# Fourteen column pairs per MLP in seven products, and their accumulated sums a product later

## The chip, the cores and the metric

The kernel runs on one core of one Trainium2 chip. A core has TensorE (PE; its weight loads are listed apart as PEld), VectorE (DVE), ScalarE (ACT), GpSimd (POOL) and SyncE (SP), which work side by side and wait for each other by semaphores. The metric is the device time of one execution in microseconds (us). The median of three runs of the kernel before is 2265.04 us (2263.68 to 2265.47).

## The reference

A decoder trunk of two layers on 256 tokens of width 2048, all in float32. Each layer adds a mixer (attention and a scan in layer 0, dilated attention in layer 1) and then an MLP:

```python
def squared_relu_mlp(h, w_up, w_down):
    u = jnp.einsum('bsd,df->bsf', h, w_up)
    return jnp.einsum('bsf,fd->bsd', jnp.square(jax.nn.relu(u)), w_down)

for layer in range(DEPTH):
    ...
    h = rms_norm(x, norm_ffn[layer])
    x = x + squared_relu_mlp(h, w_up[layer], w_down[layer])
```

`w_up` is 2048 x 8192 and `w_down` 8192 x 2048 in each layer. The change touches the MLPs alone.

## The kernel before

**Products in three parts.** Every large weight is split into a high part `whi` (a ScalarE copy) and the rest `wlo` (a VectorE subtraction), and so are the activations (`uh`, `ul` for u, the squared relu; `sh`, `sl` for sums of u). A product is three matmuls: high x high, high x rest, rest x high. Nearly all engine calls go through one helper, so the profile shows them under L71; tile names tell them apart.

**Pieces.** The work is one list, `plan`, of pieces of two k-tiles (256 rows of a weight, 512 columns, 512 KB). `run` walks it. In the iteration of piece i it first emits `low(i+2)` (VectorE's `wlo`), `fetch(i+6)` (SP's load), `high(i+3)` (ScalarE's `whi`), `add(i+4)` (a sum of weight blocks on VectorE), then what the piece before left pending (evictions), then the piece's matmuls. There are four `wlo` and five `whi` buffers. All engines work through their instructions in the order in which they were emitted.

**Up and down.** The hidden width of 8192 is 16 stripes of 512. An up unit makes one stripe of u in 8 pieces of 12 matmuls (`acc<-whi,hThi`). Behind it a side task `squared` takes relu (ScalarE), transposes (PE, `uT`), squares (ScalarE, `uf`). A second one, `operands`, splits a pair of stripes and makes the sums s1, s2. A plain down unit multiplies a pair c of stripes (c = 0 to 7) with 512 columns of `w_down` in 4 pieces of 12 matmuls (`acc<-whi,uh`).

**Seven products.** Instead of two plain down units (two column stripes of one pair c), a `Seven` takes the 2 x 2 blocks (two token tiles, two halves of the pair, two column stripes) with seven products in place of eight, in the Strassen-Winograd manner. Each product has two pieces of six matmuls (`sp<-`). Table `SEVEN` (L240) sets their order, each with its PSUM bank a, b or c and its weight block. `LOADS` says which blocks are loaded by SP with which product, `SUMS` which are summed on VectorE (`sraw<-sraw`). Two further sums (block 11 + block 12, and 12 + 22) are made by accumulating DMAs on POOL's queue, whose tile is also `sraw` (L276). A bank goes on accumulating over its products; after each product it is added to the residual (`res<-res,sp`) before the next product writes to it.

**Order.** `mixed` spreads the pieces of sevens among pieces of up units. Pair 6 and pair 7 stand last. Before, 12 sevens and 8 plain down units make up a layer: pairs 0, 1, 3, 4, 5 have two sevens each, pairs 2 and 6 one seven and two plain units, pair 7 four plain units.

**Side tasks.** A side task advances at a tick, twice per plain or up piece and once per product piece, as long as a running account of VectorE's and ScalarE's load is under `LIMIT`. A product's tick first books `HEAVY`, as much as `LIMIT`, so that no task runs there. What a piece needs and is not there yet is forced at that piece by `need`: the rest of the task's instructions are then emitted at once, ahead of the piece's matmuls.

Of the kernel before, what the change touches and what calls it, by code (L numbers as in the profile page):

```python
# [20 lines left out]
W = 512  # L21
# [19 lines left out]
def trunk(ctx: ExitStack, tc: tile.TileContext, x, norm_mix, norm_ffn, w_up, w_down, ab_w_in, ab_q_norm,  # L41
# [193 lines left out]
    def unit(*a, **k):  # L235
# [1 line left out]

    SEVEN = (("P1", "a", "11"), ("P2", "b", "21"), ("Q6", "a", "t2"), ("Q7", "c", "12"), ("Q5", "a", "11"),  # L240
             ("Q4", "c", "21"), ("Q3", "a", "22"))
    LOADS = {"P1": ("11",), "P2": ("21", "12", "22")}
    SUMS = {"Q6": ("t2", "11", "22"), "Q4": ("21", "21", "t2")}

    class Seven:


        def __init__(self, w, rows, c0, kts, operands, to, needs, mark):
            self.w, self.rows, self.c0, self.operands, self.to, self.needs, self.mark = \
                w, rows, c0, operands, to, needs, mark  # L250
# [8 lines left out]
        def fetch(self, p, h):  # L259
            for b in LOADS.get(SEVEN[p][0], ()):  # L260
                r, c = self.rows[int(b[0]) - 1] + h * KC, self.c0 + (int(b[1]) - 1) * W
                nc.sync.dma_start(self.tile(b, h),
                                  self.w[r * 128:(r + KC) * 128, c:c + W].rearrange("(k p) c -> p k c", p=128))

        def add(self, p, h):
            if SEVEN[p][0] in SUMS:
# [4 lines left out]
        def accumulate(self, p, h):  # L271

            o = {"P1": ("11", 0), "P2": ("12", 1)}.get(SEVEN[p][0])
            if o is not None:
                r, c = self.rows[o[1]] + h * KC, self.c0 + W
                nc.gpsimd.dma_start(self.raw[o[0], h],  # L276
                                    self.w[r * 128:(r + KC) * 128, c:c + W].rearrange("(k p) c -> p k c", p=128),
                                    accum_op=OP.add)

        def source(self, p, h):  # L280
            return self.raw[SEVEN[p][2], h]
# [1 line left out]
        def evict(self, p):  # L283

            name, b, _ = SEVEN[p]
            t, j, op = {"P1": (0, 0, OP.add), "P2": (0, 0, OP.add), "Q6": (1, 0, OP.add), "Q7": (1, 1, OP.subtract),
                        "Q5": (1, 1, OP.subtract), "Q4": (1, 0, OP.add), "Q3": (0, 1, OP.subtract)}[name]
            r = self.to[t][j]
            V.tensor_tensor(r, r, self.bank[b], op=op)

    def run():
        todo = plan
# [31 lines left out]
        def low(i):  # L324
            if i < len(todo):
                raw = raws.pop(i)
                lo = wpool.tile([128, KC, raw.shape[2]], F32R, name="wlo", bufs=AHEAD + 1)
                V.tensor_tensor(lo, raw, f32(parts[i][0]), op=OP.subtract)
                parts[i].append(lo)
                u, c = todo[i]  # L330
                if isinstance(u, Seven):
                    u.accumulate(*c)

        for i in range(RAW):
            if i % 2 == 0:
# [285 lines left out]
                last(t, j)  # L621
        free(ps)

    def residual_unit(w, ktiles, j, needs={}, nm=None, last=None, check=None, mark=None):
        def after(ps):
            if check is not None:
                check()
# [323 lines left out]
    def mlp(layer, nm, nxt, last=None):  # L951
# [60 lines left out]
        def down(c, j):  # L1012
            kts = [(4 * (2 * c + b) + k, (lambda b=b, k=k: u[2 * c + b] + (k,))) for b in range(2) for k in range(4)]
            marks[c].append(("down", layer, c, j))
            if c < NC - 1:
                return residual_unit(wd, kts, j, {4 * b: ("u", layer, 2 * c + b) for b in range(2)},
                                     mark=marks[c][-1]).pieces

            def whole():
                assert all(("down", layer, k, j) in done or ("down", layer, k, j - j % 2) in done for k in range(NC - 1))  # L1020

            return residual_unit(wd, kts, j, {4 * b: ("u", layer, 2 * c + b) for b in range(2)}, nxt, last, whole).pieces

        def seven(c, j):
            def parts(name):
# [5 lines left out]
            return Seven(wd, (8 * c, 8 * c + 4), j * W, 4, parts,  # L1031
                         [[res[:, t, (j + i) * W:(j + i + 1) * W] for i in range(2)] for t in range(2)],
                         {0: ("u", layer, 2 * c), 1: ("u", layer, 2 * c + 1), 2: ("sums", layer, c)},
                         marks[c][-1]).pieces

        def mixed(rest, s, start, end):

# [20 lines left out]

    n2 = Norm(R_MIX + 16, False)
    mlp(0, n1, n2)  # L1060
# [111 lines left out]
```

## Time and profile before

| | |
|---|---|
| median of 3 runs | 2265.04 us |
| profiled execution, its own time | 2264.74 us |
| its span, first to last instruction | 2262.9 us |
| PE, DVE, ACT busy in the span | 99%, 77%, 57% |
| chain of waits, share of PE | 97% |
| MLP of layer 0, about 515 to 1180 us | DVE 551.89 us busy, DMA share 0.81 |
| MLP of layer 1, about 1600 to 2263 us | DVE 540.62 us busy, DMA share 0.80 |
| granted TensorE clock | 1.00 |

A row of the timeline has its start, its duration, engine, line, operation, out<-in, the shape, a count, and in brackets the idle time of the engine before it with what ended that. Busy times of neighbouring matmuls overlap: the step from start to start tells what one costs. A row of the chain of waits has start, length and what ran.

### The profile page before, as it was taken

The page shows a single profiled execution, that of the slowest core. Times are in us where ns is not written, and L with a number is a line of the kernel's source. Part 1 is how long each engine was busy: PE and PEld are TensorE (multiplying, and loading weights), DVE is VectorE, ACT ScalarE, POOL GpSimd, SP SyncE. Part 2 cuts the span into 40 slices and gives each one's busy share as a digit, 9 for nine tenths or more (in the row PEclk, how much of TensorE's full clock was granted, in tenths as well). Part 3 has the DMA queues.
Part 4 walks back from the last instruction along what each step waited for, and adds up shares of the span by engine and source line. Part 5 has one row for each costly group of instructions (what it writes and reads, how often), then busy time and mean ns, then how long its engine had stood idle before and what let it go on. Part 6 is the DMA issues. An engine that isn't in the chain of part 4 may idle for free.

```text
span 2262.9 us, 30235 instructions
## 1 busy us (share of the span) xinstructions
PE 2247.2 (99%) x11029; PEld 1873.0 (83%) x11029; DVE 1749.7 (77%) x2482; ACT 1290.0 (57%) x1615; POOL 125.7 (6%) x116
## 2 busy tenths in 40 slices
PE   8999999999999999999999999999999999999999
PEld 7998988888888888888788778778888888888877
DVE  6779986556888888887976766665588888888786
ACT  6565545445666556565664555555566665656663
POOL 1000000000001010000000000000000000010000
PEclk9999999999999999999999999999999999999999
DMA  7546555568797797888756455546788789797874
GB/s 235 163 142 190 177 177 182 190 186 246 216 296 214 209 288 222 242 245 234 219 171 192 149 158 168 168 151 186 245 237 240 206 242 281 207 282 228 248 222 141
DMA packets 255318, 475.10 MB, mean 210 GB/s; under 512 B 17156, under 2 KB 27696, under 8 KB 255168
## 3 DMA queue, kind: packets, MB, share of 16 engines
q1 hardware_dynamic: 218976, 416.34, 56.7%
q0 software_dynamic: 26624, 50.48, 12.5%
q10 hardware_dynamic: 9568, 6.34, 0.9%
q8 instruction: 86, 1.41, 0.2%
q14 instruction: 64, 0.52, 0.1%
HBM read 470.97 MB, written 2.13 MB: 209 GB/s over the span
## 4 chain that ended last, share of the span: by engine, by line
PE 97%; DMA 1%; DVE 1%; issue 1%; ACT 0%; SPq 0%; DVEq 0%; POOLq 0%; ACTq 0%
PE acc L71 71%; PE sp L71 20%; PE uT L71 1%; PE sc L71 1%; PE o L71 1%; DMA sraw<-in_w_down_dram 1%; PE pT L71 1%; PE yp L71 1%; PE xT L71 1%; DVE wlo L71 1%; DMA wraw<-in_ab_w_in_dram 0%; PE qp L71 0%; DMA res<-in_x_dram 0%; PE yo L71 0%; PE kp L71 0%
## 5 line engine op out<-in xcount | busy, mean ns | idle before, releaser
L71 ACT ACTIVATE whi<-wraw 128x1024 fp32r<-128x1024 f32 (+1 forms) x600 | 631.9, 1054 | 493.6 <-PE acc L71 350.8
L71 DVE TENSOR_TENSOR wlo<-wraw,whi 128x1024 fp32r<-128x1024 f32 (+1 forms) x600 | 725.0, 1214 | 233.7 <-PE acc L71 159.7
L71 PE MATMUL acc<-whi,hThi 128*128 128x512 f32 (+1 forms) x1632 | 647.7, 397 | 1.8 <-ACT hThi L71 1.7
L71 PE MATMUL acc<-whi,hTlo 128*128 128x512 f32 (+1 forms) x1632 | 634.8, 389 | 1.0 <-DVE hTlo L71 1.0
L71 PE MATMUL acc<-wlo,hThi 128*128 128x512 f32 (+1 forms) x1632 | 634.1, 389 | 0.7 <-DVE wlo L71 0.7
L71 ACT ACTIVATE whi<-sraw 128x1024 fp32r<-128x1024 f32 x336 | 353.7, 1059 | 292.4 <-DVE sraw L71 137.0
L71 DVE TENSOR_TENSOR wlo<-sraw,whi 128x1024 fp32r<-128x1024 f32 x336 | 408.8, 1221 | 85.3 <-PE acc L71 35.3
L71 PEld LDWEIGHTS acc<-whi,hThi 128*128 128x128 f32 x1632 | 307.6, 188 | 66.8 <-issue 5.8
L71 PEld LDWEIGHTS acc<-whi,hTlo 128*128 128x128 f32 x1632 | 307.2, 188 | 65.7 <-DVE hTlo L71 1.8
L71 PEld LDWEIGHTS acc<-wlo,hThi 128*128 128x128 f32 x1632 | 307.9, 189 | 60.9 <-DVE wlo L71 1.1
L276 POOL DMA_DIRECT2D sraw<-in_w_down_dram x96 | 117.3, 1576 | 2058.7 <-DVE wlo L71 1815.6
L71 PE MATMUL sp<-wlo,sh 128*128 128x512 f32 x384 | 149.5, 389 | 0.0
L71 PE MATMUL sp<-whi,sl 128*128 128x512 f32 x384 | 149.5, 389 | 0.0
L71 PE MATMUL sp<-whi,sh 128*128 128x512 f32 x384 | 149.4, 389 | 0.0
L71 DVE TENSOR_TENSOR sraw<-sraw 128x1024 f32<-128x1024 f32 x96 | 117.1, 1219 | 26.4 <-DMA sraw<-in_w_down_dram 26.3
L71 DVE TENSOR_TENSOR res<-res,sp 128x512 f32<-128x512 f32 x168 | 114.7, 682 | 17.4 <-PE sp L71 17.1
L71 PE MATMUL acc<-hThi,whi 128*128 128x256 f32 x384 | 112.3, 293 | 0.0
L71 PE MATMUL sp<-whi,ul 128*128 128x512 f32 x288 | 112.1, 389 | 0.0
L71 PE MATMUL sp<-whi,uh 128*128 128x512 f32 x288 | 112.0, 389 | 0.0
L71 PE MATMUL sp<-wlo,uh 128*128 128x512 f32 x288 | 112.0, 389 | 0.0
L71 PE MATMUL acc<-hThi,wlo 128*128 128x256 f32 x384 | 108.5, 283 | 0.0
L71 PE MATMUL acc<-hTlo,whi 128*128 128x256 f32 x384 | 108.5, 283 | 0.0
(221 smaller groups left out, 2749.8 us busy)
## 6 DMA issues: line engine op xcount, KB each, us to landing
wraw<-in_w_up_dram SPq DMA_DIRECT2D x256, 512.0 KB, 5.2
sraw<-in_w_down_dram SPq DMA_DIRECT2D x192, 512.0 KB, 8.1
wraw<-in_ab_w_in_dram SPq DMA_DIRECT2D x96, 512.0 KB, 3.7
sraw<-in_w_down_dram POOLq DMA_DIRECT2D x96, 512.0 KB, 10.7
wraw<-in_c_w_qkv_dram SPq DMA_DIRECT2D x96, 512.0 KB, 4.2
wraw<-in_w_down_dram SPq DMA_DIRECT2D x64, 512.0 KB, 4.2
wraw<-in_ab_w_out_dram SPq DMA_DIRECT2D x48, 512.0 KB, 3.7
wraw<-in_c_w_o_dram SPq DMA_DIRECT2D x32, 512.0 KB, 3.6
```

The costliest lines, as they stand in the source:

```text
L71: return f(out, *a, **k)
L276: nc.gpsimd.dma_start(self.raw[o[0], h], self.w[r * 128:(r + KC) * 128, c:c + W].rearrange("(k p) c -> p k c", p=128), accum_op=OP.add)
```

## The change

Per layer 14 sevens (two for each of the pairs 0 to 6) and four plain down units (pair 7) take the place of 12 and 8. Further:

- The order of the products becomes P1, P2, Q7, Q6, Q5, Q4, Q3 (Q6 and Q7 change places).
- Block 12 is loaded together with block 11, with P1, and its accumulation with block 22 is issued on POOL's queue right behind its load. Block 11 is accumulated as before, after the subtraction of P1's piece.
- `operands` of pair 6 waits for pair 5's down work, and no longer for the end of all up units.
- The last two up units' pieces and the plain units of pair 7 are mixed anew with pair 6's sevens.
- A column's last step (norm of the next stage in layer 0, store in layer 1) starts when both its plain unit of pair 7 and its seven of pair 6 are through.

```diff
-    SEVEN = (("P1", "a", "11"), ("P2", "b", "21"), ("Q6", "a", "t2"), ("Q7", "c", "12"), ("Q5", "a", "11"),
+    SEVEN = (("P1", "a", "11"), ("P2", "b", "21"), ("Q7", "c", "12"), ("Q6", "a", "t2"), ("Q5", "a", "11"),
              ("Q4", "c", "21"), ("Q3", "a", "22"))
-    LOADS = {"P1": ("11",), "P2": ("21", "12", "22")}
+    LOADS = {"P1": ("12", "11"), "P2": ("21", "22")}
...
                 nc.sync.dma_start(self.tile(b, h),
                                   self.w[r * 128:(r + KC) * 128, c:c + W].rearrange("(k p) c -> p k c", p=128))
+                if b == "12":
+                    self.accumulate("12", 1, h)
...
-                if isinstance(u, Seven):
-                    u.accumulate(*c)
+                if isinstance(u, Seven) and c[0] == 0:
+                    u.accumulate("11", 0, c[1])
...
-            for k in marks[c - 1] if 0 < c < NC - 2 else [("up", layer)] if c else []:
+            for k in marks[c - 1] if 0 < c < NC - 1 else [("up", layer)] if c else []:
                 yield from until(k)
...
+        def ready(j, stored=True):
+
+            if early[j] == 2:
+                if last is not None and stored:
+                    for t in range(2):
+                        last(t, j)
+                if nxt is not None:
+                    nxt.begin(j)
...
-        for c, n in enumerate((20, 20, 8, 20, 20, 24, 0)):
+        for c, n in enumerate((18, 17, 17, 18, 17, 17, 8)):
             x, o = ups[o:o + n], o + n
+            s = seven(c, 0) + seven(c, 2)
             if c == NC - 2:
-                x = sum((down(c, j) for j in (0, 1)), []) + sum((down(c + 1, j) for j in range(NS)), [])
-                mixed(x, seven(c, 2), 2, 19)
-            elif n == 8:
-                mixed(x + down(c, 2) + down(c, 3), seven(c, 0), 4.5, 16)
+                mixed(x, s[:9], 4, n + 4)
+                mixed(sum((down(c + 1, j) for j in range(NS)), []), s[9:], 0, 15)
             else:
-                mixed(x, seven(c, 0) + seven(c, 2), 4.5, n + (3 if n == 24 else 0))
+                mixed(x, s, 4.5, n)
```

**Where instructions move: VectorE behind the last up piece.** In the changed kernel, layer 0, Q7 (bank sp_9828), Q6 and Q5 (both in bank sp_9705) and the first pieces of pair 7 (wlo_9869, wlo_9893) stand on VectorE like this; whi_9826 with wlo_9835 is Q6's second piece, wlo_9845 and wlo_9858 belong to Q5.

```order
L71 TENSOR_TENSOR res_82<-res_82,sp_9828 128x512
L71 TENSOR_TENSOR wlo_9858<-sraw_9589,whi_9849 128x1024
L71 TENSOR_TENSOR sraw_9646<-sraw_9646,sraw_9795 128x1024
L71 TENSOR_TENSOR wlo_9869<-wraw_9824,whi_9860 128x1024
L71 TENSOR_TENSOR res_82<-res_82,sp_9705 128x512
L71 TENSOR_TENSOR wlo_9882<-sraw_9646,whi_9873 128x1024
L71 TENSOR_TENSOR sraw_9699<-sraw_9699,sraw_9807 128x1024
L71 TENSOR_TENSOR wlo_9893<-wraw_9847,whi_9884 128x1024
L71 TENSOR_TENSOR res_82<-res_82,sp_9705 128x512
L71 TENSOR_TENSOR ul_9919<-uf_9631,uh_9918 128x1024
```

Q6's eviction, which Q5's first matmul waits for, stands behind two subtractions and a sum; before, Q7 stood between Q6 and Q5.

**ScalarE at the first plain unit of pair 7.** Its operand is uh_9918; relu_9902 and uf_9905 are of the last up unit, whose squares `operands` waits for. whi_9897 is the piece three ahead of the unit's first (whi_9860). The changed kernel:

```order
L71 ACTIVATE whi_9860<-wraw_9824 128x1024
L71 ACTIVATE whi_9873<-sraw_9646 128x1024
L71 ACTIVATE whi_9884<-wraw_9847 128x1024
L71 ACTIVATE whi_9897<-sraw_9699 128x1024
L71 ACTIVATE relu_9902<-acc_9594,rs32_4976 128x512
L71 ACTIVATE relu_9902<-acc_9595,rs32_4976 128x512
L71 ACTIVATE uf_9905<-uT_9906 128x512
L71 ACTIVATE uf_9905<-uT_9912 128x512
L71 ACTIVATE uh_9918<-uf_9631 128x1024
L71 ACTIVATE uh_9928<-uf_9905 128x1024
```

The kernel before, at the first plain unit of pair 6 (whi_9686, operand uh_9729, made from squares that are there):

```order
L71 ACTIVATE whi_9686<-wraw_9641 128x1024
L71 ACTIVATE whi_9698<-wraw_9653 128x1024
L71 ACTIVATE whi_9711<-sraw_9672 128x1024
L71 ACTIVATE whi_9724<-wraw_9684 128x1024
L71 ACTIVATE uh_9729<-uf_8903 128x1024
L71 ACTIVATE relu_9733<-acc_9409,rs32_4976 128x512
L71 ACTIVATE relu_9733<-acc_9410,rs32_4976 128x512
```

Before, uh stands ahead of the relu; now it stands behind relu, two transposes and two squares.

**PE at the same place of the changed kernel.** whi_9849 is the last product piece ahead of the unit (Q5).

```order
L71 MATMUL sp_9705<-whi_9849,sh_9676 128x512
L71 MATMUL sp_9705<-wlo_9858,sh_9676 128x512
L71 MATMUL sp_9705<-whi_9849,sl_9677 128x512
L71 MATMUL uT_9906<-cst_78,relu_9902 128x128 x4
L71 MATMUL uT_9912<-cst_78,relu_9902 128x128 x4
L71 MATMUL acc_9900<-whi_9860,uh_9918 128x512
L71 MATMUL acc_9900<-wlo_9869,uh_9918 128x512
L71 MATMUL acc_9900<-whi_9860,ul_9919 128x512
```

The last up unit's transposes stand directly between that product and the unit.

More of the change, by code (lines that the diff above doesn't have):

```diff
@@ L269, in add, with accumulate @@
                 V.tensor_tensor(self.raw[o, h] if o != "t2" else self.tile(o, h), x, y, op=OP.add)
[L271 to L278, printed above, removed]
+        def accumulate(self, b, half, h):
+            r, c = self.rows[half] + h * KC, self.c0 + W
+            nc.gpsimd.dma_start(self.raw[b, h],
+                                self.w[r * 128:(r + KC) * 128, c:c + W].rearrange("(k p) c -> p k c", p=128),
+                                accum_op=OP.add)
         def source(self, p, h):
@@ L289, in evict @@
             V.tensor_tensor(r, r, self.bank[b], op=op)
+            if p == 6 and self.after is not None:
+                self.after()
     def run():
@@ L622, in add_stripe, with residual_unit @@
         free(ps)
-    def residual_unit(w, ktiles, j, needs={}, nm=None, last=None, check=None, mark=None):
+    def residual_unit(w, ktiles, j, needs={}, nm=None, last=None, mark=None):
         def after(ps):
-            if check is not None:
-                check()
             add_stripe(ps, j, last)
@@ L1017, in down, with after, sevens_end @@
                                      mark=marks[c][-1]).pieces
-            def whole():
-                assert all(("down", layer, k, j) in done or ("down", layer, k, j - j % 2) in done for k in range(NC - 1))
-            return residual_unit(wd, kts, j, {4 * b: ("u", layer, 2 * c + b) for b in range(2)}, nxt, last, whole).pieces
+            def after(ps):
+                if early[j]:
+                    add_stripe(ps, j, last)
+                else:
+                    add_stripe(ps, j)
+                early[j] += 1
+                ready(j, False)
+            return Unit([(wd, j * W, W)], kts, after,
+                        needs={4 * b: ("u", layer, 2 * c + b) for b in range(2)}).pieces
+        early = [0] * NS
+        def ready(j, stored=True):
[5 more added lines that the diff above has]
+                    nxt.begin(j)
+        def sevens_end(j):
+            for k in (j, j + 1):
+                early[k] += 1
+                ready(k)
         def seven(c, j):
@@ L1033, in seven @@
                          {0: ("u", layer, 2 * c), 1: ("u", layer, 2 * c + 1), 2: ("sums", layer, c)},
-                         marks[c][-1]).pieces
+                         marks[c][-1], (lambda: sevens_end(j)) if c == NC - 2 else None).pieces
         def mixed(rest, s, start, end):
```

6 lines of the change are left out of this document (3 added, 3 removed).

## The prediction

> **What bounds the kernel now.** I read the page first: how busy each engine is, and which chain ends last.
>
> ```profile
> span 2262.9 us, 30235 instructions
> PE 2247.2 (99%) x11029; PEld 1873.0 (83%) x11029; DVE 1749.7 (77%) x2482; ACT 1290.0 (57%) x1615; POOL 125.7 (6%) x116
> PE 97%; DMA 1%; DVE 1%; issue 1%; ACT 0%; SPq 0%; DVEq 0%; POOLq 0%; ACTq 0%
> ```
>
> TensorE is the bound, with 97% of the chain. A matmul's busy time overlaps its successor's, so its true price is its step, from long runs in the chain of waits (start, length, count) and from the windows that hold the two MLPs (length, then PE, PEld, DVE, ACT, POOL busy, clock, DMA share, GB/s).
>
> ```profile
> 394.31 29.95 PE acc L71 x132
> 515.00:1180.00 665.00, 663.67 (x3002) 548.95 (x3001) 551.89 (x546) 404.72 (x442) 58.65 (x48) 1.00 0.81 235
> 1600.00:2263.00 663.00, 656.81 (x2953) 542.22 (x2951) 540.62 (x522) 390.16 (x408) 58.60 (x48) 1.00 0.80 233
> ```
>
> 29.95 / 132 = 0.227 us per 128x512 matmul. VectorE's 551.89 of 665 is 83%: second, with room. So the time moves by matmuls removed and by places where PE waits. Last I asked the timeline where PE waits inside the MLPs. In each layer the first plain down unit does so; PE rows of layer 0, then of layer 1:
>
> ```profile
> 1081.49 0.39 PE L71 MATMUL sp<-whi,sl 128*128 128x512 f32 x1
> 1082.62 0.50 PE L71 MATMUL acc<-whi,uh 128*128 128x512 f32 x1 [0.74 <-ACT uh L71]
> 1082.96 0.39 PE L71 MATMUL acc<-wlo,uh 128*128 128x512 f32 x1
> 1083.94 0.50 PE L71 MATMUL acc<-whi,ul 128*128 128x512 f32 x1 [0.59 <-DVE ul L71]
> 2170.97 0.39 PE L71 MATMUL sp<-whi,sl 128*128 128x512 f32 x1
> 2172.09 0.50 PE L71 MATMUL acc<-whi,uh 128*128 128x512 f32 x1 [0.74 <-ACT uh L71]
> ```
>
> Beyond the step PE loses 1082.62 - 1081.49 - 0.23 = 0.90 us for uh and 1083.94 - 1082.96 - 0.23 = 0.75 for ul: 1.65 per layer.
>
> **The change, part 1: fewer matmuls.** A pair of plain columns costs 2 units x 8 k-tiles x 2 token tiles x 3 = 96 matmuls, seven products 7 x 4 x 3 = 84. Two more such pairs per layer, two layers: 4 x 12 = 48 matmuls, 48 x 0.227 = **-10.9 us**, all on the bound engine.
>
> **Part 2: what they add elsewhere.** Each exchange adds 6 pieces to split (14 instead of 8), 4 weight sums, 3 evictions and 4 accumulating DMAs. The steps of VectorE and ScalarE come from starts that follow each other:
>
> ```profile
> 1067.93 1.22 DVE L71 TENSOR_TENSOR sraw<-sraw 128x1024 f32<-128x1024 f32 x1
> 1068.12 0.39 PE L71 MATMUL acc<-whi,hThi 128*128 128x512 f32 x1
> 1069.07 0.68 DVE L71 TENSOR_TENSOR res<-res,sp 128x512 f32<-128x512 f32 x1
> 1069.27 1.06 ACT L71 ACTIVATE whi<-sraw 128x1024 fp32r<-128x1024 f32 x1 [1.24 <-DVE sraw L71]
> 1069.66 1.22 DVE L71 TENSOR_TENSOR wlo<-wraw,whi 128x1024 fp32r<-128x1024 f32 x1
> ```
>
> A 128x1024 subtraction or sum keeps VectorE 1.14 us (67.93 to 69.07), an eviction 0.59; from a sum's start to the split that reads it pass 1.34. So 4 x (10 x 1.14 + 3 x 0.59) = 53 us more VectorE and 4 x 6 copies more ScalarE. They hide under PE: one up piece with two pieces of products is 24 x 0.227 = 5.45 us of PE against 3 x 1.14 + 0.65 (8 sums per 28 pieces) + 0.59 = 4.66 on VectorE, 86%. I count nothing; were that cover gone, VectorE would set each such group.
>
> **Part 3: the stall at the old place goes.** Its units become products, and the split of their u starts a stage earlier: 2 x 1.65 = **-3.3 us**.
>
> **Part 4: a longer stall at a new place.** The first plain unit now reads u of pair 14/15, and stands six pieces of products behind the last up piece. Ticks of products run no side task, so that whole chain (relu, transposes, squares, split) stands at the unit itself, behind the ScalarE split of piece whi_9897, which waits for a sum on VectorE. Also Q5 now follows Q6 directly there, both in bank sp_9705, so Q5 waits for Q6's eviction. Prices of the chain, from two stretches of the timeline:
>
> ```profile
> 1081.53 1.04 ACT L71 ACTIVATE uh<-uf 128x1024 fp32r<-128x1024 f32 x1
> 1082.47 1.25 ACT L71 ACTIVATE relu<-acc,rs 128x512 f32<-128x512 f32 x2
> 1082.67 1.22 DVE L71 TENSOR_TENSOR ul<-uf,uh 128x1024 fp32r<-128x1024 f32 x1
> 1843.98 0.39 PE L71 MATMUL sp<-whi,sl 128*128 128x512 f32 x1
> 1844.21 0.60 PE L71 MATMUL uT<-cst,relu 128*128 128x128 f32 x4
> 1844.40 0.69 DVE L71 TENSOR_TENSOR res<-res,sp 128x512 f32<-128x512 f32 x1 [0.29 <-PE sp L71]
> 1844.56 0.48 PE L71 MATMUL acc<-whi,uh 128*128 128x512 f32 x1
> 1844.84 0.60 ACT L71 ACTIVATE uf<-uT 128x512 f32<-128x512 f32 x1
> 1845.34 1.05 ACT L71 ACTIVATE whi<-wraw 128x1024 fp32r<-128x1024 f32 x1
> ```
>
> A copy of 128x1024 keeps ScalarE 0.94; the two relus end 1.25 after they start; four transposes keep PE 0.35, and the square follows 0.63 after their start, the next ScalarE step 0.50 later; uh's start to the unit's first matmul is 1.09 (1081.53 to 1082.62); an eviction starts 0.19 after the product's last step.
>
> Take the start of the last up piece as 0. An up piece is 2.72 us, a product piece 1.36, so Q7 ends at 5.44 and Q6 at 8.16. VectorE is at its best held by its four wlo buffers; it evicts Q7 at 5.63, and then in the order shown ahead: wlo_9858 at 6.22, sum sraw_9646 at 7.36, wlo_9869 at 8.50, Q6's eviction at 9.64. Q5 can start at 9.64 + 0.68 = 10.32 and ends at 13.04. VectorE goes on: wlo_9882 at 10.23, sum sraw_9699 at 11.37. ScalarE: whi_9897 at 11.37 + 1.34 = 12.71, relus 13.65 to 14.90, first square 0.52 later (three transposes are left then) at 15.42, second 15.92, uh 16.42, first matmul of the unit 17.51. Without waits it would start at 10.88 + 2 x 0.35 = 11.58. That is 5.9 us, and the wait for ul behind it stays 0.75: **6.7 us per layer, +13.4**.
>
> From below: if VectorE had nothing else, Q6's eviction ends at 9.03, Q5h0 at 10.39 frees whi_9897's buffer, and the same chain reaches the unit at 15.19: 3.6 + 0.75 = 4.4 per layer, 8.7. From above: VectorE has been late with an eviction today:
>
> ```profile
> 816.66 0.39 PE L71 MATMUL sp<-whi,sh 128*128 128x512 f32 x1
> 820.37 0.68 DVE L71 TENSOR_TENSOR res<-res,sp 128x512 f32<-128x512 f32 x1
> ```
>
> This one (Q6's) ended 4.39 us after the next piece had started. As late as 2.7 us beyond my chain makes 9.4 per layer, 18.8. I take 13.4, since buffers, not guesses, fix its start.
>
> **Part 5: more room for the accumulated sums.** Waits of VectorE for them, and the two late subtractions that PE felt:
>
> ```profile
> DVE sraw L71 <- DMA sraw<-in_w_down_dram: 26.3, 17, 4.3
> 1901.10 0.39 PE L71 MATMUL acc<-whi,hThi 128*128 128x512 f32 x1
> 1902.16 0.50 PE L71 MATMUL acc<-wlo,hThi 128*128 128x512 f32 x1 [0.67 <-DVE wlo L71]
> 2202.60 0.39 PE L71 MATMUL acc<-whi,uh 128*128 128x512 f32 x1
> 2203.40 0.50 PE L71 MATMUL acc<-wlo,uh 128*128 128x512 f32 x1 [0.42 <-DVE wlo L71]
> q0 software_dynamic: 26624, 50.48, 12.5%
> ```
>
> VectorE waited 26.3 us, but of it PE felt at most 0.83 + 0.57 = 1.4, the rest lies under its lead of three pieces. Between 0 and 1.4, I take **-0.7**. The 16 added accumulations (96 now) raise q0's share by about a sixth, 2% of the span; the windows above have 19% of the DMA engines' time free to hide it. P1's own block now queues behind another load; six pieces of lead (over 10 us) cover that.
>
> **Part 6: the end of the stage.** Norm and stores of a column now start when both its down unit and its seven are through. The third column's norm so begins one down piece before the end; its operand is needed at the fifth piece of the next unit, 4 x 2.72 = 10.9 us after that end, and it takes eight transposes, four copies and four subtractions of the size in this row of the groups (count, busy, mean ns, idle):
>
> ```profile
> L71 ACT ACTIVATE hThi<-xT,gains 128x256 fp32r<-128x256 f32 x64 | 26.0, 463 | 0.1
> ```
>
> Four times 0.46 us lie under PE's pieces: nothing. If they did not, PE would wait some 2 us once, since layer 1 has no norm behind it.
>
> **Sum.** -10.9 - 3.3 + 13.4 - 0.7 = -1.5. The profiled execution took 2264.74 (its span and 1.84 around it), 0.3 under the median of 2265.04; so 2263.2 like with like, **2263.5** against the median. A difference under 0.2%, 4.5 us, cannot be told from none here. From the bounds: -10.9 - 3.3 + 8.7 - 1.4 = -6.9 and -10.9 - 3.3 + 18.8 = +4.6, so 2258.5 to 2269.5 for this case alone.
>
> **The rivals.** *The new stall costs no more than the old one* (1.65 per layer): -10.9 - 0.7 = -11.6, 2253.5. For it: ScalarE is 57% busy and could be ahead. Against: the two waits stand in its queue and in PE's by program order, whatever the load. Chance 0.12.
>
> *The shared bank stalls the other sevens too.* Q5 follows Q6 through bank a in all 28; in 26 an up or down piece of 2.72 us stands between. It decides from an eviction that ends later than that. At 1069.07 above one stands directly behind a sum, as Q6's now will, and ends 1069.75 - 1068.12 = 1.63 after the next piece began: it fits. The one at 820.37 would not: 4.39 - 2.72 = 1.7 us. If a third of the 26 were late by that, 15 us: 2278. Against: that lateness came with the late accumulations that get more room. Chance 0.13.
>
> *The clock gate.* At the program's start matmuls of 128x288 step at 0.24 us, later at 0.13, until PE had worked for some 6 us (7.98 to 13.97):
>
> ```profile
> 13.25 0.44 PE L71 MATMUL acc<-wlo,hThi 128*128 128x288 f32 x1
> 13.49 0.44 PE L71 MATMUL acc<-whi,hTlo 128*128 128x288 f32 x1
> 18.32 0.29 PE L71 MATMUL acc<-whi,hTlo 128*128 128x288 f32 x1
> 18.45 0.30 PE L71 MATMUL acc<-whi,hThi 128*128 128x288 f32 x1
> ```
>
> If the new stall brought the slow step back for 6 us, each layer would lose 6 x (1 - 0.13 / 0.24) = 2.7, 5.4 in all: 2269. Against: no gap of my chain is over 2.2 us (8.16 to 10.32), and the windows' granted clock is 1.00. The Trainium skill, page "TensorE: Matmul & The Clock Gate", section "HAM oscillation — how this bites in real kernels", sets the limit at PE gaps over about 3.4 us; by that rule the forecast stands as long as no single gap passes it, and the slow start in the rows above agrees with its cold state. Chance 0.05.
>
> **Chances.** Forecast 0.70, the rivals 0.12, 0.13, 0.05. The forecast's own tails give 0.03 to faster and 0.02 to slower, the clock gate 0.01 to slower: faster 0.15, same 0.69, slower 0.16. With 0.25 on the outer rivals the range must reach into both: down to a new stall of 3.7 us per layer (2257.5), up to evictions late in four or five of the 26 places (4 x 1.7 = 7 us, 2270.5, and a little): **2257.5 to 2271.5**.
>
> **What would show it.** 48 matmuls fewer at the same step; no wait for uh at the first down unit's old place; in each layer one cluster of PE gaps of 6 to 7 us between the last up piece and the next plain unit, released by VectorE's eviction, ScalarE's relu and uh, and ul; VectorE's wait for accumulations well under 26.3; no new PE waits on res in the other sevens. I am wrong if that cluster is under 4 us or over 9.5 per layer, or if PE waits elsewhere by more than 3 us.

## The result, and the profile after

The changed kernel takes **2365.33 us** (median of 4 runs, 2362.71 to 2365.93) against 2264.81 (4 runs) for the kernel before: ratio 1.0444, 95% interval 1.0431 to 1.0456. It is 100 us slower, where the prediction said no difference.

The page of the changed kernel, the rows that answer those of before: the span, the busy times, and the shares of the chain that ended last. Then the windows of its two MLPs (length, PE, PEld, DVE, ACT, POOL busy, clock, DMA share, GB/s).

```profile
span 2363.7 us, 30362 instructions
PE 2282.1 (97%) x10981; PEld 1885.4 (80%) x10981; DVE 1803.2 (76%) x2534; ACT 1308.6 (55%) x1639; POOL 143.3 (6%) x132
PE 80%; DMA 15%; DVE 3%; ACT 1%; issue 1%; SPq 0%; ACTq 0%; DVEq 0%
```

```profile
515.00:1225.00 710.00, 676.16 (x2946) 550.14 (x2945) 573.52 (x560) 409.13 (x442) 67.41 (x56) 0.97 0.79 225
1640.00:2363.70 723.70, 684.58 (x2978) 557.83 (x2976) 572.21 (x553) 404.29 (x425) 67.42 (x56) 0.97 0.78 222
```

In the MLPs the granted clock is 0.97 in place of 1.00, and the DMA share no higher than before. The 48 matmuls are gone (11029 to 10981), and so is TensorE's hold on the chain: 97% to 80%, with 15% for transfers that had 1%. Where they stand is told by the chain of waits in order of time (start, length, what ran); these are its pieces of over 18 us that are transfers, the first three and the last two of 14:

```profile
533.35 21.57 DMA wraw<-in_w_up_dram
633.34 22.04 DMA wraw<-in_w_up_dram
727.50 22.22 DMA wraw<-in_w_up_dram
...
2150.80 21.58 DMA wraw<-in_w_up_dram
2241.40 21.32 DMA sraw<-in_w_down_dram
```

One comes with each group of two sevens, some 95 us apart: a load of 512 KB that takes 18.5 to 22.2 us from its issue to its landing. The timeline of ScalarE and then of TensorE shows what the second one does.

```profile
642.22 1.07 ACT L71 ACTIVATE whi<-sraw 128x1024 fp32r<-128x1024 f32 x1 [1.23 <-DMA sraw<-in_w_down_dram]
650.27 1.06 ACT L71 ACTIVATE whi<-sraw 128x1024 fp32r<-128x1024 f32 x1 [6.98 <-DMA sraw<-in_w_down_dram]
655.48 1.06 ACT L71 ACTIVATE whi<-wraw 128x1024 fp32r<-128x1024 f32 x1 [4.15 <-DMA wraw<-in_w_up_dram]
```

```profile
652.64 0.50 PE L71 MATMUL sp<-wlo,uh 128*128 128x512 f32 x1 [0.76 <-DVE wlo L71]
653.69 0.40 PE L71 MATMUL sp<-whi,ul 128*128 128x512 f32 x1
656.59 0.80 PE L71 MATMUL acc<-whi,hThi 128*128 128x512 f32 x1 [2.50 <-ACT whi L71]
657.85 0.80 PE L71 MATMUL acc<-wlo,hThi 128*128 128x512 f32 x1 [0.47 <-DVE wlo L71]
658.44 0.63 PE L71 MATMUL acc<-whi,hTlo 128*128 128x512 f32 x1
658.87 0.63 PE L71 MATMUL acc<-whi,hThi 128*128 128x512 f32 x1
```

ScalarE waits 7.0 and 4.2 us for blocks and weights, eats up the lead of its copies, and TensorE stands. Behind the gap the matmuls follow each other at 0.43 us (658.44 to 658.87) in place of 0.227: the clock has gone down as well. The waits of ScalarE for these two kinds of loads, over the whole run, before and then after (us in total, times, longest):

```profile
ACT whi L71 <- DMA sraw<-in_w_down_dram: 41.6, 36, 2.6
ACT whi L71 <- DMA wraw<-in_w_up_dram: 14.0, 12, 3.4
```

```profile
ACT whi L71 <- DMA sraw<-in_w_down_dram: 105.4, 33, 7.2
ACT whi L71 <- DMA wraw<-in_w_up_dram: 59.7, 16, 5.8
```

**Where the 100.8 us of span are** (2262.9 to 2363.7), added up over the starts of all recorded matmuls from 540 us on: 48 matmuls fewer, -10.9; matmuls at the slow clock's step of 0.43 us, some +26 (about 130 of them); waits ahead of matmuls and transposes, the rest, some +86. Of these waits the place at pair 7, which the prediction spoke of, has 8.0 and 8.2 us in the two layers less the old stall of 3.3. Some 73 us are new: about 5 in each of the 14 groups of sevens.

**Why the loads take 22 us.** The same stretch of the program, before and after: the issue of each 512 KB transfer and its landing, from the trace's records of transfers (only some are listed).

```
before                                     after
SP   block    629.77 -> 640.62             SP   block    629.56 -> 642.14
SP   block    631.03 -> 641.97             SP   block    630.07 -> 646.18
SP   block    632.48 -> 644.82             SP   block    630.72 -> 650.16
SP   up       633.80 -> 647.66             SP   block    631.78 -> 654.10
SP   up       635.15 -> 651.61             SP   up       633.34 -> 655.38
POOL accum.   637.37 -> 646.65             POOL accum.   632.26 -> 641.95
POOL accum.   641.92 -> 650.97             POOL accum.   635.12 -> 645.90
POOL accum.   642.65 -> 654.98             POOL accum.   639.68 -> 649.96
POOL accum.   643.38 -> 659.62             POOL accum.   643.33 -> 653.93
```

While accumulations are under way, POOL's and SP's transfers land in turn, one pair every 4.0 us (642.14, 646.18, 650.16, 654.10). Without them SP's loads land every 1.3 us (before: 639.31, 640.62, 641.97). Before, the taking of turns began when all but one of the seven's blocks had landed; now it begins with block 21 and 22 still to come, and the up weights queue behind them. The DMA view of 40 us (620 to 660, slices of 1 us) has it as bytes; the changed kernel:

```profile
DMA  0058300879999999999999999999999999999828
GB/s 0 0 115 268 141 0 0 131 262 387 309 385 305 377 420 387 354 276 262 250 262 270 262 248 266 272 262 248 266 272 262 246 277 397 412 406 397 297 55 143
q0 software_dynamic: 1088, 2.10, 28.3%
```

The engines are full from 629 to 657, and move some 260 GB/s while accumulations run, against 305 to 420 in the slices of 629 to 636 and some 400 behind.

### The profile page after: what moved, and what is told of

The parts are those of the page before. It is cut to its first block, busy times and chain, and to the rows that moved or that the text cites. A ratio compares the mean times of both kernels' runs of the same rounds, so it can differ in the third digit from the quotient of the medians.

```text
span 2363.7 us, 30362 instructions
## 1 busy us (share of the span) xinstructions
PE 2282.1 (97%) x10981; PEld 1885.4 (80%) x10981; DVE 1803.2 (76%) x2534; ACT 1308.6 (55%) x1639; POOL 143.3 (6%) x132
## 3 DMA queue, kind: packets, MB, share of 16 engines
q0 software_dynamic: 30976, 58.87, 14.0%
## 4 chain that ended last, share of the span: by engine, by line
PE 80%; DMA 15%; DVE 3%; ACT 1%; issue 1%; SPq 0%; ACTq 0%; DVEq 0%
PE acc L71 56%; PE sp L71 19%; DMA wraw<-in_w_up_dram 12%; DMA sraw<-in_w_down_dram 2%; DVE wlo L71 2%; PE sc L71 1%; PE o L71 1%; PE uT L71 1%; PE pT L71 1%; ACT whi L71 1%; PE yp L71 1%; PE xT L71 1%; DVE res L71 0%; DMA wraw<-in_ab_w_in_dram 0%; DVE ul L71 0%
## 5 line engine op out<-in xcount | busy, mean ns | idle before, releaser
L71 DVE TENSOR_TENSOR wlo<-wraw,whi 128x1024 fp32r<-128x1024 f32 (+1 forms) x568 | 687.4, 1215 | 260.2 <-PE acc L71 150.3
L71 ACT ACTIVATE whi<-wraw 128x1024 fp32r<-128x1024 f32 (+1 forms) x568 | 597.3, 1053 | 455.7 <-PE acc L71 267.3
L71 ACT ACTIVATE whi<-sraw 128x1024 fp32r<-128x1024 f32 x392 | 412.5, 1059 | 421.9 <-DVE sraw L71 129.3
L71 DVE TENSOR_TENSOR wlo<-sraw,whi 128x1024 fp32r<-128x1024 f32 x392 | 475.8, 1222 | 125.7 <-ACT whi L71 71.1
L71 PE MATMUL sp<-whi,sh 128*128 128x512 f32 x448 | 177.0, 395 | 9.5 <-DVE res L71 9.5
L71 PE MATMUL sp<-wlo,sh 128*128 128x512 f32 x448 | 177.0, 395 | 1.1 <-DVE wlo L71 1.1
L71 PE MATMUL sp<-whi,sl 128*128 128x512 f32 x448 | 176.5, 394 | 0.0
L71 PE MATMUL sp<-wlo,uh 128*128 128x512 f32 x336 | 132.6, 395 | 7.0 <-DVE wlo L71 6.9
L71 PE MATMUL sp<-whi,uh 128*128 128x512 f32 x336 | 131.8, 392 | 4.4 <-ACT whi L71 4.4
L71 PEld LDWEIGHTS sp<-whi,sh 128*128 128x128 f32 x448 | 86.2, 192 | 29.3 <-ACT whi L71 9.1
```

The source lines that it names most:

```text
L71: return f(out, *a, **k)
```

## The experiments

Twelve kernels, in four groups, each with its own runs of the kernel before beside it (2264.2 to 2264.5), to which the ratios are. The changed kernel's loss is called 100 us.

**1. The changed kernel with the old order and the old loads.**

```diff
-    SEVEN = (("P1", "a", "11"), ("P2", "b", "21"), ("Q7", "c", "12"), ("Q6", "a", "t2"), ("Q5", "a", "11"),
+    SEVEN = (("P1", "a", "11"), ("P2", "b", "21"), ("Q6", "a", "t2"), ("Q7", "c", "12"), ("Q5", "a", "11"),
...
-    LOADS = {"P1": ("12", "11"), "P2": ("21", "22")}
+    LOADS = {"P1": ("11",), "P2": ("21", "12", "22")}
...
-                if b == "12":
-                    self.accumulate("12", 1, h)
...
                     u.accumulate("11", 0, c[1])
+                if isinstance(u, Seven) and c[0] == 1:
+                    u.accumulate("12", 1, c[1])
```

> The change with its fourteen sevens and its new end of the stage, but with the order of products, the loads and the accumulations of the kernel before (block 12 loaded with P2, accumulated behind P2's subtraction). Theory 1, the early accumulations of block 12 hold up the loads of P2's blocks and PE's long waits then bring the slow clock: the stalls at P2 go, what stays is 48 matmuls less (-10.9), the old stall less (-3.3) and the new one at pair 7 (about 8 per layer in the changed kernel, somewhat less here since Q7 again stands between Q6 and Q5): 2258 to 2268. Rival, fourteen sevens with fewer up pieces between them are too dense for the DMA engines and VectorE: the stalls stay, 2330 or more.

Measured 2303.98, ratio 1.0182 (1.0165 to 1.0199): between the two. Undoing the order and the loads gives back 61 of the 100 us, but 14 sevens with the old order lose 40 of their own. VectorE's wait for accumulations, which the changed kernel no longer has, is three times what it was before (26.3):

```profile
DVE sraw L71 <- DMA sraw<-in_w_down_dram: 77.2, 43, 3.5
```

**2. The kernel before with the new order, the new loads and the early accumulation of block 12**, its 12 sevens and their places kept.

```diff
-    LOADS = {"P1": ("11",), "P2": ("21", "12", "22")}
+    LOADS = {"P1": ("12", "11"), "P2": ("21", "22")}
...
+                if b == "12":
+                    self.accumulate("12", 1, h)
...
-                    u.accumulate(*c)
+                    u.accumulate("11", 0, c[1])
```

> The kernel before with its twelve sevens and its mixing, and only the new order of products, loads and accumulations. Theory 1: one stall at P2 for the first seven of each group, some five to seven groups per layer, 5 to 8 us each with the slow clock: 2320 to 2360. Rival (density): 2264 to 2270, since the mixing is the old one.

Measured 2354.0, ratio 1.0396 (1.0375 to 1.0416). The same products and the same 96 accumulations as before, only in another order and at other moments, cost 90 us. So 14 sevens are not needed for the loss. This kernel alone does not part the moment of the transfers from the new order of products: 32.8 us of TensorE's waits in it are for evictions. The third kernel parts them.

**3. The changed kernel without the accumulation of block 22 into block 12.**

```diff
-                if b == "12":
-                    self.accumulate("12", 1, h)
```

> The changed kernel without the accumulation of block 22 into block 12 (Q7 then multiplies a wrong weight, and 56 of 112 accumulating transfers are left out); all else as in the change. Theory 1: the stalls at P2 go, 2260 to 2272 with the stall at pair 7 left. Rival (density of loads by SP and of VectorE's work, which stay): 2330 or more.

It leaves out 56 of 112 accumulations, so Q7 has a wrong weight. Measured 2264.81, ratio 1.0000 (0.9990 to 1.0011). The whole loss goes with them. The chain is TensorE's again, and at pair 7 TensorE's waits stand as the prediction named them (layer 0):

```profile
PE 98%; DVE 1%; DMA 1%; ACT 1%; SPq 0%; issue 0%; ACTq 0%; DVEq 0%
1092.62 0.47 PE L71 MATMUL sp<-whi,sh 128*128 128x512 f32 x1 [2.16 <-DVE res L71]
1096.54 0.33 PE L71 MATMUL uT<-cst,relu 128*128 128x128 f32 x1 [0.96 <-ACT relu L71]
1099.79 0.79 PE L71 MATMUL acc<-whi,uh 128*128 128x512 f32 x1 [1.68 <-ACT uh L71]
```

**4. The same accumulation later**, behind the subtraction of P1's piece with the same rows, just ahead of block 11's.

```diff
-                if b == "12":
-                    self.accumulate("12", 1, h)
...
                 if isinstance(u, Seven) and c[0] == 0:
+                    u.accumulate("12", 1, c[1])
                     u.accumulate("11", 0, c[1])
```

> The changed kernel with block 12's accumulation issued behind the subtraction of P1's piece, just ahead of block 11's, in place of right behind its load: some 7 us later. Theory 1 in its strict form (what matters is that P2's loads are through first): 2262 to 2275. If instead any accumulation of block 12 ahead of P2 is too early, or Q7 as the third product comes before its block is ready: 2300 or more, with waits of ScalarE for block 12 at Q7.

Measured 2334.56, ratio 1.0310 (1.0289 to 1.0330): 31 us back, 70 still lost. A little later helps a little; P2's loads have not landed by then either.

**5. The changed kernel with a plain transfer in place of block 12's accumulation**, which overwrites 12 with 22 (Q7 has a wrong weight).

```diff
-                                accum_op=OP.add)
+                                **({} if b == "12" else {"accum_op": OP.add}))
```

> The changed kernel, except that the transfer of block 22 on POOL's queue at block 12's tile is a plain one: it overwrites 12 instead of being added to it, so Q7 gets a wrong weight. Same number of transfers, same bytes read and written by them, same places in the queue. Theory A (the added-up kind is what is dear: a transfer that must read its target back before it writes holds the DMA engines longer, and SP's loads land every 4.0 us beside it): with the plain kind SP's loads land every 2 to 3 us while POOL's are in flight, TensorE's waits in the groups of sevens mostly go, 2266 to 2300 us. Theory B (any transfer on POOL's queue at that moment takes turns with SP's in-order loads, whatever its kind): loads still land every 4.0 us, 2350 us or more.

Measured 2307.95, ratio 1.0195 (1.0178 to 1.0212). It is theory A for 57 of the 100 us, but not for all: 43 stay lost with plain transfers in that place, while without any transfer there (the third kernel) nothing is lost. What POOL's queue holds of the 16 DMA engines stands in the page's rows by queue (packets, MB, share); of the changed kernel, of the third kernel and of this one:

```profile
q0 software_dynamic: 30976, 58.87, 14.0%
```

```profile
q0 software_dynamic: 15744, 29.51, 7.5%
```

```profile
q0 software_dynamic: 23808, 58.87, 10.7%
```

The first gives 0.140 x 2363.7 / 112 = 2.95 us of all 16 engines for one accumulation, the second 0.075 x 2263.9 / 56 = 3.0. In the third, 56 of these make 167 of 247 us, which leaves 1.4 for a plain transfer of the same bytes. So adding doubles what a transfer costs. The same rows give 272 packets for an accumulation ((30976 - 15744) / 56) and 144 for a plain transfer ((23808 - 15744) / 56), of the same bytes.

The sign that theory A named, loads landing every 2 to 3 us, is met in part only. In one stretch (from the trace's records of transfers) SP's loads land at 631.56, 635.64, 636.80 and 638.68 us beside two plain transfers, and at 642.64 and 646.04 beside block 11's accumulations. Loads still take up to 19.9 us in this kernel.

**6. The first kernel, with side tasks allowed at pair 6's products.**

```diff
+            self.light = after is not None
...
-                tick(True)
+                tick(not u.light)
```

> The kernel with 14 sevens and the old order of products, loads and accumulations, and side tasks may also advance at the products of pair 6, so the relu, squares and split for pair 7 are not all left to the first plain unit. If the forecast was right that this chain stalls TensorE because no task runs at those products: the clusters of gaps between the last up piece and pair 7 (some 8 and 10 us in the two layers without this edit) fall to under 4 us, and the kernel takes 8 to 14 us less than the 2304.0 without it: 2288 to 2297. If the stall came from late weights or late evictions there, not from the tasks: within 3 us of 2304.

Measured 2298.22, ratio 1.0148 (1.0133 to 1.0163): 5.8 us less, short of 8. The relu comes earlier: TensorE's waits for it fall from 8.9 to 4.4 us in total. But its two waits for uh at pair 7 rise from 3.3 to 7.8 (4.7 and 3.1), so the clusters do not fall under 4. In front of uh ScalarE now waits for a product (1.9 us) and for a sum on VectorE (1.5 us). Program order is a part of that stall; how large a part is not shown.

**7 and 8. No accumulating transfers: POOL adds the blocks itself**, 112 sums of 128x1024 on blocks that SP loads; old order. The second also has the ticks of the sixth kernel, by the same two lines.

```diff
-            nc.gpsimd.dma_start(self.raw[b, h],
-                                self.w[r * 128:(r + KC) * 128, c:c + W].rearrange("(k p) c -> p k c", p=128),
-                                accum_op=OP.add)
+            a = self.raw[o, h]
+            nc.gpsimd.tensor_tensor(a, a, self.raw[x, h], op=OP.add)
```

> 14 sevens, old order of products; no accumulating transfers at all. Blocks 11, 12 are loaded by SP with P1, 21 and 22 with P2; the sums 11 + 12 and 12 + 22 are made by POOL with a tensor_tensor of 128x1024, behind the products' subtractions. Theory (accumulating transfers among the loads are the whole loss; the 48 matmuls fewer are a real gain): no cluster of PE gaps in the groups of sevens, only the pair-7 stall of some 6 us per layer stays: 2258 to 2270. Rival 1 (14 sevens leave VectorE and the buffers too little room, whatever feeds them): 2285 or more with PE waiting for wlo in the sevens. Rival 2 (POOL's sums are too slow or get in VectorE's way: a 128x1024 sum on POOL takes over 3 us, VectorE's sums and subtractions get longer than 1.22 us while POOL works): PE waits on sraw and wlo, 2290 or more.

> As the kernel with POOL's sums, and side tasks may advance at the products of pair 6 as well. If the pair-7 stall goes as well: 6 to 12 us under the kernel with POOL's sums alone; with the theory's time for that, 2248 to 2262. If the stall has another cause: within 3 us of it.

Measured 2410.58, ratio 1.0647 (1.0631 to 1.0663), and 2404.93, 1.0617 (1.0602 to 1.0633). Rival 2 holds. The groups of operations (count, busy, mean ns, idle) of the first, then of the kernel before:

```profile
L274 POOL TENSOR_TENSOR sraw<-sraw 128x1024 f32<-128x1024 f32 x112 | 350.6, 3151 | 2003.1 <-DVE wlo L71 1822.0
L71 DVE TENSOR_TENSOR wlo<-sraw,whi 128x1024 fp32r<-128x1024 f32 x392 | 572.4, 1475 | 33.8 <-issue 25.5
L71 DVE TENSOR_TENSOR sraw<-sraw 128x1024 f32<-128x1024 f32 x112 | 179.9, 1606 | 0.0
```

```profile
L71 DVE TENSOR_TENSOR sraw<-sraw 128x1024 f32<-128x1024 f32 x96 | 117.1, 1219 | 26.4 <-DMA sraw<-in_w_down_dram 26.3
```

A sum keeps POOL 3.15 us, and VectorE's own sums grow from 1.22 to 1.61 us. The Trainium skill, page "SBUF — State Buffer", section "Who interferes with whom", states that a VectorE instruction with two inputs in SBUF contends with a GpSimd instruction that reads SBUF; these rows agree. VectorE's busy time rises to 2016.8 us, and TensorE waits for wlo. The eighth kernel is 5.7 us under the seventh, just short of the 6 that were expected.

**9. The changed kernel with that sum on VectorE**: one entry more in the table of sums, and no accumulation of block 12.

```diff
-    SUMS = {"Q6": ("t2", "11", "22"), "Q4": ("21", "21", "t2")}
+    SUMS = {"Q6": ("t2", "11", "22"), "Q4": ("21", "21", "t2"), "Q7": ("12", "12", "22")}
...
-                if b == "12":
-                    self.accumulate("12", 1, h)
```

> The changed kernel with its order of products and loads, but the sum 12 + 22 is made by VectorE (56 sums more, 1.14 us each) in place of POOL's accumulating transfers; 56 of the 112 accumulations stay (block 11). Theory (the accumulating transfers are the loss, through the DMA engines): as the kernel that left these accumulations out, 2264.8, if VectorE's 64 us more hide under TensorE; 2260 to 2272. Rival (VectorE has no such room: 573 of 710 us in the MLP before, then some 605 of 665, 91%): waits on wlo and sraw in the sevens, 2280 or more.

Measured 2269.87 (9 runs), ratio 1.0023 (1.0013 to 1.0033). The theory holds: 95 of the 100 us come back, and the whole computation is done. VectorE's 56 sums cost 5.1 us over the kernel that leaves them out. Some 4 of them stand in the first group of sevens of each layer, where TensorE now waits 0.6 us for wlo and 1.3 for an eviction beyond its step. Windows of this kernel: the MLP of layer 0, and 8 us at pair 7 (length, PE, PEld, DVE, ACT, POOL busy, clock, DMA share, GB/s); then TensorE's waits just ahead of them:

```profile
515.00:1180.00 665.00, 658.24 (x2957) 543.55 (x2955) 603.52 (x588) 410.36 (x447) 33.72 (x28) 0.99 0.71 218
1100.00:1108.00 8.00, 6.28 (x16) 4.40 (x15) 3.94 (x4) 3.90 (x6) 0.00 (x0) 0.57 0.59 224
```

```profile
1094.83 0.47 PE L71 MATMUL sp<-whi,sh 128*128 128x512 f32 x1 [2.24 <-DVE res L71]
1098.75 0.33 PE L71 MATMUL uT<-cst,relu 128*128 128x128 f32 x1 [0.94 <-ACT relu L71]
1101.99 0.79 PE L71 MATMUL acc<-whi,uh 128*128 128x512 f32 x1 [1.68 <-ACT uh L71]
```

VectorE is busy 603.52 of 665 us, 91%, and TensorE still leads. The stall at pair 7 is as in the third kernel, and the clock falls behind it (0.57).

**10. The sixth kernel with the same sum on VectorE.** Old order, block 11 still accumulated.

```diff
+    SUMS = {"Q6": ("t2", "11", "22"), "Q4": ("21", "21", "t2"), "Q7": ("12", "12", "22")}
...
-                if isinstance(u, Seven) and c[0] == 1:
-                    u.accumulate("12", 1, c[1])
```

> 14 sevens with the old order of products and the old loads, side tasks allowed at pair 6's products, and the sum 12 + 22 made by VectorE. Against the same kernel with accumulating transfers (2298.2). If late and slow accumulations are what is left of that kernel's loss: 2250 to 2265, and VectorE's wait for them (76 us there) falls under 20. If it is the denser spacing of 14 sevens: 2280 or more.

Measured 2309.42, ratio 1.0202 (1.0188 to 1.0216): my theory for it falls. VectorE's timeline tells why:

```profile
DVE sraw L71 <- DMA sraw<-in_w_down_dram: 76.7, 42, 3.6
1003.81 1.23 DVE L71 TENSOR_TENSOR sraw<-sraw 128x1024 f32<-128x1024 f32 x1 [2.62 <-DMA sraw<-in_w_down_dram]
1007.83 1.23 DVE L71 TENSOR_TENSOR sraw<-sraw 128x1024 f32<-128x1024 f32 x1 [1.07 <-DMA sraw<-in_w_down_dram]
```

Both sums start as block 11's accumulations land (1003.78 and 1007.81, 9.1 and 9.5 us after their issue). Q6 needs the sum of block 11, with 12 added, and 22. In the old order Q6 is the third product, and with 17 or 18 up pieces to a group in place of 20 it comes, as I read it, too soon. In the ninth kernel, with Q7 ahead of Q6, VectorE never waits for an accumulation. So the new order, with the loads that go with it, keeps VectorE from these waits. That 14 sevens need it is argued, not shown: the ninth and tenth kernels differ in order, loads and side tasks at once.

**11. The kernel before, with the sum 12 + 22 on VectorE**, by the same entry in its table of sums.

```diff
-            o = {"P1": ("11", 0), "P2": ("12", 1)}.get(SEVEN[p][0])
+            o = {"P1": ("11", 0)}.get(SEVEN[p][0])
```

> The kernel before with its 12 sevens, and the sum 12 + 22 made by VectorE: 48 accumulating transfers fewer, 48 sums more. Says what these transfers cost the kernel before. VectorE waited 26.3 us for accumulations there and TensorE felt some 1.4 of it, so 2255 to 2264 if that is all that they cost; over 2268 if VectorE cannot take the sums.

Measured 2266.96 (11 runs), ratio 1.0011 (1.0002 to 1.0021). That is 2.5 us above the kernel before, and above the 2255 to 2264 expected. Taking 48 accumulations out and putting 48 sums on VectorE gains nothing. The sums have a price (56 cost 5.1 us in the ninth kernel), so this kernel alone does not show that the accumulations cost nothing at their old moment, only that they cost little.

**12. The ninth kernel with the end of the up work laid out anew.**

```diff
-        for c, n in enumerate((18, 17, 17, 18, 17, 17, 8)):
+        for c, n in enumerate((17, 17, 17, 17, 17, 17, 10)):
...
-                mixed(x, s[:9], 4, n + 4)
+                mixed(x, s[:9], 4, n)
...
+                          **({4: ("u", layer, 2 * c + 2)} if c == NC - 2 and j == 0 else {})},
...
+            if i // 2 == NC - 1:
+                side(half(i))
```

`half` splits one stripe of pair 7 as a task of its own; the line with `{4: ...}` forces stripe 14's at product Q5.

> As the kernel with the changed order and the sum 12 + 22 on VectorE (2269.9), and the end of the up work is laid out anew: groups of 17 up pieces each and 10 for the last, so that the last up piece stands between Q6 and Q5; the split of stripe 14 is a task of its own, emitted two products ahead of the first unit of pair 7, and relu, squares and split of stripe 15 follow under that unit's first two pieces. If the forecast's reading of the stall is right (TensorE waits there for a chain that stands in program order, and for Q6's eviction): the cluster of 6.2 us per layer falls under 1.5 us, the slow clock behind it goes as well, and the kernel takes 10 to 17 us less, 2253 to 2260, under the kernel before. If that place is bound by late weights or by VectorE's load (91% of its time in the MLP), the gaps come back elsewhere and it stays within 4 us of 2269.9.

Measured **2260.92** (11 runs), ratio 0.9985 (0.9976 to 0.9994): 8.9 us under the ninth kernel, a little less than expected, and 3.4 under the kernel before. This is the only one that beats both. The wait for Q6's eviction and the one for stripe 14 are gone; what is left at pair 7 is a wait for stripe 15, whose transposes stand directly ahead of the unit's third piece. With the wait for ul it makes some 2.7 us per layer, over the 1.5 expected, and the slow clock still follows it (steps of 0.43 us from 1108.62 on, 2.8 us in both layers). Of the 8.9 us some 7 are waits saved at pair 7. Its rows:

```profile
1106.78 0.50 PE L71 MATMUL acc<-whi,uh 128*128 128x512 f32 x1 [1.77 <-ACT uh L71]
1108.03 0.79 PE L71 MATMUL acc<-whi,ul 128*128 128x512 f32 x1 [0.53 <-DVE ul L71]
```

## Why the prediction was wrong, and where it was right

**Parts 1 and 3 hold.** 48 matmuls are gone at the same step, and no wait for uh stands at the old place any more.

**Part 2 holds nearly.** VectorE's added work was counted as free. In the third kernel, with all of that work in it, TensorE's waits for evictions are the two at pair 7:

```profile
PE sp L71 <- DVE res L71: 4.3, 2, 2.2
```

The ninth shows the edge of the cover: 64 us more on VectorE cost 5.1.

**Part 4 holds in mechanism and in size.** The forecast was 6.7 us per layer, of it 2.16 (8.16 to 10.32) for Q6's eviction. Beyond the matmul step, the third kernel has 2.3 + 1.1 + 0.5 + 1.8 + 0.4 = 6.1 in layer 0 and 6.4 in layer 1. With late loads, as in the changed kernel, it is 8.0 and 8.2, within the bounds of 4.4 and 9.4, since the eviction is later:

```profile
1143.32 0.52 PE L71 MATMUL sp<-whi,sh 128*128 128x512 f32 x1 [4.18 <-DVE res L71]
1150.98 0.50 PE L71 MATMUL acc<-whi,uh 128*128 128x512 f32 x1 [1.68 <-ACT uh L71]
```

The twelfth kernel confirms what it is made of: another order there takes more than half of it away. The upper bound of 9.4 adds 2.7 us, which its rows do not give: the eviction at 4.39 is 2.2 us later than the chain's 2.16.

**Part 5 is the step that failed**, in two sentences. "The windows above have 19% of the DMA engines' time free to hide it" took a mean over 665 us for the stretch in which the added transfers stand. In that stretch the engines had nothing free, before or after (length, PE, PEld, DVE, ACT, POOL busy, clock, DMA share, GB/s; first before, then after):

```profile
625.00:655.00 30.00, 30.00 (x138) 24.86 (x137) 25.73 (x26) 17.66 (x20) 4.88 (x4) 1.00 1.03 307
```

```profile
625.00:655.00 30.00, 28.07 (x124) 22.32 (x122) 20.28 (x21) 13.91 (x15) 4.81 (x4) 1.00 0.98 278
```

And "six pieces of lead (over 10 us) cover that" priced the load that P1's block queues behind, 1.3 us, and not the accumulations that were moved ahead of P2's loads. Two of them at 4.0 - 1.3 = 2.7 us, and then block 11's two as well, put 11 us into SP's queue, which lands in order: loads of 22 us against that lead.

How much lead there was, the other kernels tell. Of the 512 weight loads that SP issues for the MLPs none takes over 18 us before and in the third, ninth and twelfth kernels (the longest 17.3 to 17.5), and TensorE's waits in their groups of sevens come to 4 us or less. In the fifth, fourth, second and changed kernels 26, 38, 56 and 63 do, and 43, 70, 90 and 100 us are lost. The first and tenth have 2 and 0 and lose 40 and 45: there VectorE waits 77 us for accumulations.

Part 5's other half was right: the 26.3 us of VectorE's waits for accumulations went to nothing.

The Trainium skill, page "DMA: Bandwidth & Descriptors", section "Issuing engines are not separate DMA queues", states that transfers started by different engines run on the same 16 DMA engines and interleave. The trace agrees, with its pairs of landings every 4.0 us. It was the rule to weigh against part 5, and I passed it over.

**Part 6** met nothing that contradicts it.

**The rivals.** None had late loads. The clock gate (0.05) came true through stalls that the rival did not have: some 26 us in the changed kernel. It also came true at pair 7 as the rival said, though with no gap over 2.3 us: the third kernel loses 3.1 us to the slow step, nearly all of it there, where the rival named 5.4. The shared bank (0.13) did not decide in the changed kernel, where TensorE waits three times for an eviction; in the second kernel it shows beside the late loads. The changed kernel, then the second:

```profile
PE sp L71 <- DVE res L71: 9.5, 3, 4.2
```

```profile
PE sp L71 <- DVE res L71: 32.8, 18, 3.0
```

**The sum of the other terms** was -1.5. The third kernel, without the moved accumulations, stands at +0.65 (2264.81 against 2264.16; by its interval -2.3 to +2.5), and the slow steps of 3.1 us that the sum left out are in it. With the measured sizes the terms are -10.9 - 3.3 + 12.5 - 1.4 + 3.1 = 0.0 (the two late subtractions of 1.4 are gone). So the forecast fits a kernel without the moved transfers, and it is not luck: term by term the sum stands within 1 us, the slow clock aside.

**What stays open.** 43 us are lost with plain transfers at the same moment, which hold the engines half as long. Late loads go with them (26 over 18 us), but how the engines divide their time between the two queues was not measured. The slow clock's part of each loss could not be tried apart from the waits.

## What to carry to other kernels

A transfer that is issued earlier is not just nearer to being done: it takes DMA time from the loads ahead of which it now runs, and a queue that lands in order hands the delay to everything behind. Read the DMA engines' share in the 30 us in which the moved transfers stand, not over the stage, and price the loads behind them by the landing times that the trace shows while both queues are busy. When a change adds work to one engine and moves transfers too, run it once without the transfers: here that one run separated 100 us of loss from a sum that held.

## What the runs showed of the hardware that was not expected

An accumulating transfer of 512 KB held the DMA engines 2.95 to 3.0 us in 272 packets, a plain one in the same queue 1.4 us in 144. Beside SP's loads each accumulation adds 2.7 us to the queue.

The clock fell behind clusters of gaps without a long one among them. In the ninth kernel TensorE's idle gaps ahead of 1102 us are 2.24, 0.94, 0.25 and 1.68, and the granted clock from 1100 to 1108 is 0.57; in the changed kernel the stretch behind 656 us follows gaps of 0.76 and 2.50. So the prediction's test, that no single gap passes some 3.4 us, was too weak a guard. Each such place cost 1.5 to 2 us of slow steps on top of its wait.
